# A fifth set of half products for queries and decays of heads 2 to 5, turned by transposes

## The chip, the cores and the metric

The kernel runs on one core of a Trainium2 chip. The metric is device time in microseconds (us) from start to end of one execution; of several runs the median is given. TensorE (PE in the rows) multiplies matrices, VectorE (DVE) and ScalarE (ACT) work element by element, GpSimd (POOL) does small vector work and starts transfers, SyncE (SP) starts transfers.

## What is computed

A decoder trunk of two layers on 512 positions with 2048 features. The first layer (a convolution branch and a latent-attention branch) is not touched. The second one is touched: one input projection, a gated linear recurrence (HGRN2) of 16 heads with a state of 128x128, an output projection, and the final norm.

```
p = h @ od_w_in[j]
q, f_raw, i_val, g = _split(p, [HGRN_FDIM, HGRN_FDIM, D_MODEL, D_MODEL])
o = hgrn2(q, f_raw, i_val, lb_all[l], hgrn_norm_g[j]) * jax.nn.silu(g)
x = x + o @ od_w_out[j]
```

In `hgrn2` each head has a query q, a decay that comes from f_raw through a sigmoid and a lower bound (so that the key is one minus the decay), and values i_val. Its output is a masked product of queries and keys with decays between them, plus what the state carries, normalised for each head and multiplied by the gate path of g.

## The kernel before

**Matmuls.** Every fp32 operand is split into a high and a low part (`split_plain`, `split_scaled`), and `mm3` (L223) makes one product of three matmuls: high by high, high by low, low by high. `dense` (L239) makes one result tile of 128 features by 512 positions from 16 blocks of 128 input features: four quarters of 12 matmuls. After each quarter `tick()` runs the hooks and lets every open chain take one step. A tick is thus the unit of the interleave: the order of TensorE's instructions is the order in which the program is written (`manual_schedule` for PE), while the tile framework orders the other engines itself.

**Sets of half products.** For values (`oi`) and gates (`og`) of the second layer, the 16 heads' columns are made in four sets (`SETS`) of 1024 columns each, by a scheme with seven products of half-size blocks in place of eight (`product`, `result`, the loop over `s_`, L936). One set is 7 products of 48 matmuls; the operands are sums and differences of blocks of the weights, formed on VectorE and ScalarE from blocks loaded into a ring (`ws`, tile `rw`). Here a result has positions in rows and features in columns, and is written to HBM (`vd`, `gd`).

**Heads.** Queries (`oq`) and decays (`of`) come from `dense`, so with features in rows. Heads 0 and 1 are made before the sets and kept in HBM (`qd`); heads 2 to 15 are made after the sets, one head each eight ticks, straight into SBUF: q into a tile with two buffers, the decay's key kn by turns into the tile kn and the tile m (`qk_tiles`).

**Chains.** `hgrn(h, ...)` (L1039) is the recurrence of one head, written as a generator with a `yield` for each tick that it lets pass. In order: f, products of f over groups of 4 (pi, xe; L1042 to L1054) and reciprocals; queries and keys scaled (qb, rc, X, ks; L1064 to L1078); the first product (L1082) and its masked copy into `at` (L1083); a first group of strip products (L1031) with masked copies (L1002), scaling of X (L1035) and ks (L1037); a second such group; transposes of the scaled keys (L1095); products with the values (L1101, L1111, L1113); norm, gate (L1127), and transposes back (L1131). The last step splits the head's output for the output projection.

`begin_chain` (a hook) starts the next chain when its head is projected and 8 to 10 ticks have passed; it loads the head's gate and values (`start`) as it starts. `SPREAD` places parts of the output projection (`w_out`, which adds each product to the residual xall, L671) between the dense results of heads 6 to 12; two more parts stand at the end.

**Loads.** Weight tiles of the heads' stage (`Loaded`) take two transfers from GpSimd's queue for each two quarters: the tile itself (wh), and once more added onto its negated high part (wl). Gates, values, residual and results go through SyncE's queue, which takes them in order.

Of the kernel before, what the change touches and what calls it, by code (L numbers as in the profile page):

```python
# [7 lines left out]
F32 = mybir.dt.float32  # L8
# [3 lines left out]
AF = mybir.ActivationFunctionType  # L12
# [3 lines left out]
P = 128  # L16
S = 512
# [8 lines left out]
RATE = 0.67  # L26
RATE0 = 0.4
MAN = "PE"
N_WTILES = 224
N_EARLY = 128  # L30
LAST = 2 * N_WTILES - NK
SETS = [("oi", 0), ("oi", 1), ("og", 0), ("og", 1)]


V_EVG, V_ODG, V_FING = 0, 16, 32
# [14 lines left out]
def trunk(ctx: ExitStack, tc: tile.TileContext, x, w, ws, vec, cst, rope, msk, out, order):  # L50
    nc = tc.nc
# [19 lines left out]
    def tmp(name="t", bufs=None):  # L71
        if name == "c":
            return tpc[0].tile([P, S], F32, name=name, tag=tpc[1])
        return tp.tile([P, S], F32, name=name, tag=name, bufs=bufs)
# [4 lines left out]
    def spawn(gen):  # L79
        chains.append(gen)  # L80
        return gen
# [157 lines left out]
    def dense(name, col, h, nk=NK):  # L239
        ps = ps_mm()  # L240
        for q in range(nk // 4):
            quarter(ps, next_quarter((name, col, q)), h, q, nk)
            tick()
        return ps
# [68 lines left out]
    with tc.tile_pool(name="x0", bufs=1) as x0:  # L313
# [29 lines left out]
        ident = cs[:, 0:P]  # L343
# [302 lines left out]
    def load_xa(src):  # L646
        for k in range(NK):
            nc.sync.dma_start(xa[k], src[:, k, :])
            yield
            yield  # L650
# [28 lines left out]
    h1 = []  # L679
# [86 lines left out]
    def decay(h, ps, kn):  # L766

        z = tmp("z")
        dve.tensor_tensor(out=z, in0=ps, in1=rb1, op=ALU.mult)
        t = tmp("th", bufs=1)  # L770
        act.activation(t, z, AF.Tanh, scale=0.5)
        act.activation(kn, t, AF.Identity, scale=la[:, h:h + 1], bias=nla[:, h:h + 1])
        return kn
# [91 lines left out]
            split_scaled(u[:, j, :H], vs[:, V_ODG + k:V_ODG + k + 1], h1[k][0][:, H:], h1[k][1][:, H:])  # L865


    qd = [dr.tile([P, 2, S], F32, name=f"qd{h}") for h in range(2)]
    for h in range(2):
        ps = dense("oq", h, h1)  # L870
        if h == 0:
            for k in range(4):
                x_sums(k)
            finish(c1)
        z = tmp("z")
        act.activation(z, ps, AF.Copy)
        nc.sync.dma_start(qd[h][:, 0, :], z)
        ps = dense("of", h, h1)
        if h == 0:
            for k in range(4, 8):  # L880
                x_sums(k)
            xctx.close()
            xtx.close()
            ph.append(sctx.enter_context(tc.tile_pool(name="ph", bufs=1, reuse_waits="tile")))
        nc.sync.dma_start(qd[h][:, 1, :], decay(h, ps, tp.tile([P, S], F32, name="gate", tag="gate", bufs=2)))
# [30 lines left out]
    vd = [dr.tile([P, 4, S], F32, name=f"vd{g}") for g in range(4)]  # L916
    gd = [dr.tile([P, 4, S], F32, name=f"gd{g}") for g in range(4)]

    def result(s_, col, b, in0, in1):

        name, a = SETS[s_]
        o = tp.tile([P, S], F32, name="z", tag="z") if b % 2 == 0 else tp.tile([P, S], F32, name="gate", tag="gate", bufs=2)
        dve.tensor_tensor(out=o, in0=in0, in1=in1, op=ALU.add)
        if name == "oi":
            act.activation(o, o, AF.Copy, scale=r1[:, b:b + 1])
        else:

            t = tmp("th", bufs=1)
            act.activation(t, o, AF.Tanh, scale=rh[:, b:b + 1])
            dve.scalar_tensor_tensor(out=o, in0=t, scalar=1.0, in1=o, op0=ALU.add, op1=ALU.mult)  # L930
        nc.sync.dma_start((vd if name == "oi" else gd)[2 * a + col][:, b, :], o)
# [1 line left out]
    def keep(tag, b):  # L933
        return ph[0].tile([P, S], F32, name=tag, tag=f"{tag}{b}")

    for s_ in range(4):  # L936
        p1, p2 = banks(), banks()
        for m in range(4):
            product(p1, "A11", m)
# [26 lines left out]
            result(s_, 1, b, p3[b], u[b])  # L966
        for b in range(2):
            result(s_, 1, 2 + b, p7[b], u[b])
        if s_ == 3:
            restore()  # L970
        p4 = banks()
        for m in range(4):
# [10 lines left out]
    def hgt(name, shape=(P, S), tag=None):  # L983
        return hg.tile(list(shape), F32, name=name, tag=tag or name)
# [54 lines left out]
    def hgrn(h, kn, q, gate, vr):  # L1039
# [49 lines left out]
        ab2 = hgt("ab2", (P, 4, 8))  # L1089
        yield from radix4(at, X, ks, t32, 32, ab2, P + 192)  # L1090
        yield
        yield
        pt = ps_x()
        for g in range(3):
            pe.transpose(pt[:, blocks(g)], ks[:, blocks(g)], ident)  # L1095
# [39 lines left out]
    heads = []  # L1135
    qk = {}

    def qk_tiles(h):
        qk[h] = (hg.tile([P, S], F32, name="q", tag="q", bufs=2), tmp("m", bufs=1) if h % 2 else hgt("kn"))
        return qk[h]  # L1140

    def start(h):
        gate = tp.tile([P, S], F32, name="gate", tag="gate", bufs=2)
# [3 lines left out]
        q, kn = qk[h]  # L1147
        heads.append(spawn(hgrn(h, kn, q, gate, vr)))

    for h in range(2):  # L1150
        for i, t in enumerate(qk_tiles(h)):
            nc.sync.dma_start(t, qd[h][:, i, :])


    SPREAD = {0: [(6, 1, 3), (7, 0, 3), (7, 1, 3), (8, 0, 3), (8, 1, 2), (9, 0, 2)],
              1: [(9, 1, 3), (10, 0, 3), (10, 1, 3), (11, 0, 3), (11, 1, 2), (12, 0, 2)]}
    begun = [2]
    since = [99]

    def begin_chain():  # L1160
        since[0] += 1
        n = len(heads)
        if n < begun[0] and since[0] >= (8 if n < 5 else 10 if n < 12 else 8):
            since[0] = 0
            start(n)

# [9 lines left out]
                    w_out("ow", list(range(4 * g, 4 * g + 4)), range(c, c + part[2]))  # L1176
                c += part[2]

    for h in range(2, 16):
        if h == 4:  # L1180
            spawn(load_xa(xd))
        ps = dense("oq", h, h1)
        q, kn = qk_tiles(h)
        act.activation(q, ps, AF.Copy)
        out_part(h, 0)
        decay(h, dense("of", h, h1), kn)
        begun[0] = h + 1
        out_part(h, 1)
    w_out("ow", [8, 9, 10, 11], range(NK))
# [87 lines left out]
def _weights(inp, order):  # L1277
# [26 lines left out]
        w[n // 2, :, n % 2] = b.transpose(1, 0, 2)  # L1304
    ws = np.zeros((len(SETS), 2, 2, 4, P, 2, S), np.float32)
    for n, (name, a) in enumerate(SETS):
        c0 = {"oi": 4096, "og": 6144}[name] + a * 1024

        b = od[:, c0:c0 + 1024].reshape(2, 4, 2, P, 2, S)
        ws[n] = b.transpose(0, 4, 1, 3, 2, 5)  # L1310
    return w.reshape(N_WTILES, P, 2 * S), ws.reshape(len(SETS), 2, 2, 4, P, 2 * S)

# [26 lines left out]
```

## Time and profile before

| what | us |
|---|---|
| median of 3 runs | 1762.09 |
| their range | 1756.79 to 1762.53 |
| profiled execution | 1758.25 |
| its span, first to last instruction | 1756.5 |
| TensorE busy / VectorE / ScalarE / GpSimd | 1732.9 / 1175.9 / 744.8 / 228.2 |

Stages by the trace: up to some 800 us the first layer, then heads 0 and 1, the four sets from about 860 to 1148, the heads up to about 1680, and the end. A row of the timeline has the start (us from the span's start), the duration, the engine, the line of kernel.py, the operation, output<-input, shapes and count; in brackets idle time of the engine before it and what ended it. Several instructions of one kind in a row may be merged into one row (x8: the passes of four fp32 products). The duration of a matmul runs from its start to its modelled end; since matmuls are pipelined, what one costs is read from start to start.

### The profile page before, as it was taken

The page shows a single profiled execution, that of the slowest core. Times are in us where ns is not written, and L with a number is a line of the kernel's source. Part 1 is how long each engine was busy: PE and PEld are TensorE (multiplying, and loading weights), DVE is VectorE, ACT ScalarE, POOL GpSimd, SP SyncE. Part 2 cuts the span into 40 slices and gives each one's busy share as a digit, 9 for nine tenths or more (in the row PEclk, how much of TensorE's full clock was granted, in tenths as well). Part 3 has the DMA queues.
Part 4 walks back from the last instruction along what each step waited for, and adds up shares of the span by engine and source line. Part 5 has one row for each costly group of instructions (what it writes and reads, how often), then busy time and mean ns, then how long its engine had stood idle before and what let it go on. Part 6 is the DMA issues. An engine that isn't in the chain of part 4 may idle for free.

```text
span 1756.5 us, 22385 instructions
## 1 busy us (share of the span) xinstructions
PE 1732.9 (99%) x8227; PEld 1437.6 (82%) x8227; DVE 1175.9 (67%) x2301; ACT 744.8 (42%) x1361; POOL 228.2 (13%) x307
## 2 busy tenths in 40 slices
PE   8999999999999999999999999999999999999997
PEld 6888888888888888887788888888888888888896
DVE  8554948494879885575777778876465555446656
ACT  6434444444342233275555455533433333333354
POOL 6000000000000000052000000022222222222200
PEclk9999999999999999999999999999999999999998
DMA  6222222222273223268777776798777787877642
GB/s 235 96 89 83 87 92 89 96 85 90 87 243 108 96 96 102 85 193 244 240 221 218 239 216 216 214 276 178 163 173 167 165 179 162 179 173 169 150 133 96
DMA packets 101805, 273.35 MB, mean 156 GB/s; under 512 B 9536, under 2 KB 31296, under 8 KB 101312
## 3 DMA queue, kind: packets, MB, share of 16 engines
q1 hardware_dynamic: 74048, 172.39, 29.3%
q0 software_dynamic: 27072, 98.58, 26.3%
q8 instruction: 64, 1.05, 0.3%
q10 hardware_dynamic: 576, 0.97, 0.2%
q14 instruction: 45, 0.37, 0.1%
HBM read 250.93 MB, written 20.97 MB: 155 GB/s over the span
## 4 chain that ended last, share of the span: by engine, by line
PE 92%; DVE 3%; issue 2%; DMA 2%; ACT 1%; POOL 0%; POOLq 0%; DVEq 0%; ACTq 0%
PE mm L225 25%; PE mm L227 25%; PE mm L226 25%; PE aux L1031 2%; PE aux L226 2%; PE aux L225 2%; PE aux L227 2%; PE aux L461 1%; PE aux L1082 1%; PE aux L1111 1%; DVE hl L249 1%; DMA rw<-ws 1%; PE aux L1113 1%; PE aux L1101 1%; DVE wq L253 1%
## 5 line engine op out<-in xcount | busy, mean ns | idle before, releaser
L252 ACT ACTIVATE wq<-raw 128x512 fp32r<-128x512 f32 x256 | 160.9, 631 | 346.2 <-PE mm L227 332.3
L225 PE MATMUL mm<-hh,wq 128*128 128x512 f32 x656 | 263.1, 401 | 1.1 <-ACT wq L252 1.1
L253 DVE TENSOR_TENSOR wq<-raw,wq 128x512 fp32r<-128x512 f32 x256 | 183.5, 719 | 120.2 <-ACT wq L252 119.6
L227 PE MATMUL mm<-hh,wq 128*128 128x512 f32 x656 | 257.5, 392 | 2.8 <-DVE wq L253 2.8
L226 PE MATMUL mm<-hl,wq 128*128 128x512 f32 x656 | 256.7, 391 | 0.0
L225 PE MATMUL mm<-hh,wh 128*128 128x512 f32 x512 | 207.8, 406 | 0.0
L227 PE MATMUL mm<-hh,wl 128*128 128x512 f32 x512 | 200.3, 391 | 0.0
L226 PE MATMUL mm<-hl,wh 128*128 128x512 f32 x512 | 199.6, 390 | 0.0
L510 DVE SCALAR_TENSOR_TENSOR y<-u,cwh,y 128x512 f32<-128x512 f32 x240 | 178.2, 747 | 2.4
L170 ACT ACTIVATE wl<-wh 128x1024 fp32r<-128x1024 f32 x86 | 91.5, 1064 | 178.4 <-PE mm L227 169.8
L227 PEld LDWEIGHTS mm<-hh,wq 128*128 128x128 f32 x656 | 123.8, 189 | 30.4 <-DVE wq L253 3.9
L225 PEld LDWEIGHTS mm<-hh,wq 128*128 128x128 f32 x656 | 124.3, 190 | 27.2 <-ACT wq L252 2.0
L226 PEld LDWEIGHTS mm<-hl,wq 128*128 128x128 f32 x656 | 124.2, 189 | 26.0 <-DVE hl L249 0.5
L227 PEld LDWEIGHTS mm<-hh,wl 128*128 128x128 f32 x512 | 96.1, 188 | 21.2 <-DMA wl<-w 0.4
L226 PEld LDWEIGHTS mm<-hl,wh 128*128 128x128 f32 x512 | 96.4, 188 | 17.8
L225 PEld LDWEIGHTS mm<-hh,wh 128*128 128x128 f32 x512 | 96.4, 188 | 17.5
L671 DVE TENSOR_TENSOR xall<-xall,mm 128x512 f32<-128x512 f32 x96 | 65.7, 684 | 64.3 <-PE mm L227 64.3
L252 ACT ACTIVATE wh<-rw 128x1024 fp32r<-128x1024 f32 x66 | 69.8, 1058 | 79.4 <-PE aux L227 23.7
L225 PE MATMUL mm<-mh,wq 128*128 128x512 f32 x256 | 101.6, 397 | 0.0
L226 PE MATMUL mm<-ml,wq 128*128 128x512 f32 x256 | 101.3, 396 | 0.0
L227 PE MATMUL mm<-mh,wq 128*128 128x512 f32 x256 | 101.2, 395 | 0.0
L253 DVE TENSOR_TENSOR wl<-rw,wh 128x1024 fp32r<-128x1024 f32 x66 | 79.8, 1221 | 20.2 <-ACT wh L252 6.0
(317 smaller groups left out, 3575.7 us busy)
## 6 DMA issues: line engine op xcount, KB each, us to landing
raw<-w SPq DMA_DIRECT2D x127, 512.0 KB, 3.3
rw<-ws SPq DMA_DIRECT2D x96, 512.0 KB, 4.7
wh<-w POOLq DMA_DIRECT2D x86, 512.0 KB, 3.7
wl<-w POOLq DMA_DIRECT2D x86, 512.0 KB, 6.2
ts<-ws POOLq DMA_DIRECT2D x16, 512.0 KB, 5.8
xall<-xT SPq DMA_DIRECT2D x16, 256.0 KB, 5.2
xd<-xall SPq DMA_DIRECT2D x16, 256.0 KB, 2.5
vr<-vd SPq DMA_DIRECT2D x16, 256.0 KB, 4.3
```

Source lines behind the costliest of these rows:

```text
L170: act.activation(self.lo, self.hi.bitcast(F32), AF.Copy, scale=-1.0)
L225: pe.matmul(ps, a[0][:, asl], b[0][:, bsl], start=first, stop=False)
L226: pe.matmul(ps, a[0][:, asl], b[1][:, bsl], start=False, stop=False)
L227: pe.matmul(ps, a[1][:, asl], b[0][:, bsl], start=False, stop=last)
L249: dve.scalar_tensor_tensor(out=lo, in0=src, scalar=g, in1=hi.bitcast(F32), op0=ALU.mult, op1=ALU.subtract)
L252: act.activation(hi, src, AF.Copy)
L253: dve.tensor_tensor(out=lo, in0=src, in1=hi.bitcast(F32), op=ALU.subtract)
L461: pe.matmul(po[:, jb * P:], vr[:, jb, blocks(j)], pts[jb], start=jb == 0, stop=jb == 3)
L510: dve.scalar_tensor_tensor(out=y, in0=u[:, j:j + S], scalar=cwh[:, w0 + j:w0 + j + 1], in1=y, op0=ALU.mult, op1=ALU.add)
L671: dve.tensor_tensor(out=xa[c], in0=xa[c], in1=ps, op=ALU.add)
L1031: pe.matmul(ps[:, i * 192:(i + 1) * 192], ks[:, blocks(g)], rhs, start=True, stop=True)
L1082: pe.matmul(ps[:, blocks(g)], kb[:, blocks(g)], qb[:, blocks(g)], start=True, stop=True)
```

## The change

`SETS` gets a fifth entry `qf`: the columns of queries and decays of heads 2 to 5. Its results (positions in rows) go to a new HBM tensor `qs`, queries as they are, decays after a tanh on ScalarE. Their dense results fall away, and with them 16 of the 224 weight tiles. When such a head is due, `load_qk` loads its two tiles and three ticks later `turn_qk` turns them: four 128x128 transposes each on TensorE, and a copy by ScalarE (for the decay with its scale and bias).

Dense results after the sets begin with head 6. Heads 6 to 13 now go to HBM (`qd`) and come back by `load_qk`; heads 14 and 15 stay in SBUF. kn is one tile for all of these. A chain begins 7 ticks after the one before, at the earliest 4 ticks after its load. One `yield` between the second group of strip products and the transposes of the keys is gone. `SPREAD` moves to heads 10 to 13.

```diff
-N_WTILES = 224
+N_WTILES = 208
-SETS = [("oi", 0), ("oi", 1), ("og", 0), ("og", 1)]
+SETS = [("oi", 0), ("oi", 1), ("og", 0), ("og", 1), ("qf", 0)]
+ENTRY = (0, 1)
...
     def result(s_, col, b, in0, in1):
...
+        if name == "qf":
+            if col:
+                act.activation(o, o, AF.Tanh, scale=rh[:, b:b + 1])
+            nc.sync.dma_start(qs[col][:, b, :], o)
+            return
...
-    for s_ in range(4):
+    for s_ in range(len(SETS)):
...
         yield from radix4(at, X, ks, t32, 32, ab2, P + 192)
         yield
-        yield
         pt = ps_x()
...
-    def qk_tiles(h):
-        qk[h] = (hg.tile([P, S], F32, name="q", tag="q", bufs=2), tmp("m", bufs=1) if h % 2 else hgt("kn"))
-        return qk[h]
+    def load_qk(h):
+        qk[h] = (hg.tile([P, S], F32, name="q", tag="q", bufs=2), hgt("kn"))
+        if not 2 <= h < 6:
+            for i, t in enumerate(qk[h]):
+                nc.sync.dma_start(t, qd[h][:, i, :])
+            return
+        rows.extend((tmp("z"), tmp("m", bufs=1)))
+        for i, t in enumerate(rows):
+            nc.sync.dma_start(t.rearrange("p (b c) -> p b c", b=4), qs[i][:, :, blocks(h - 2)])
+
+    rows = []
+
+    def turn_qk(h):
+
+        for i, t in enumerate(rows):
+            pt = ps_x()
+            for b in range(4):
+                pe.transpose(pt[:, blocks(b)], t[:, blocks(b)], ident)
+            if i == 0:
+                act.activation(qk[h][0], pt, AF.Copy)
+            else:
+                act.activation(qk[h][1], pt, AF.Identity, scale=la[:, h:h + 1], bias=nla[:, h:h + 1])
+        rows.clear()
...
-    SPREAD = {0: [(6, 1, 3), (7, 0, 3), (7, 1, 3), (8, 0, 3), (8, 1, 2), (9, 0, 2)],
-              1: [(9, 1, 3), (10, 0, 3), (10, 1, 3), (11, 0, 3), (11, 1, 2), (12, 0, 2)]}
-    begun = [2]
-    since = [99]
+    SPREAD = {0: [(10, 1, 4), (11, 0, 6), (11, 1, 6)],
+              1: [(12, 0, 4), (12, 1, 4), (13, 0, 8)]}
+    begun = [6]
+    loaded = [0]
+    since = [9]
 
     def begin_chain():
         since[0] += 1
         n = len(heads)
-        if n < begun[0] and since[0] >= (8 if n < 5 else 10 if n < 12 else 8):
+        loaded[0] += 1
+        if n not in qk and n < begun[0] and since[0] >= 3:
+            load_qk(n)
+            loaded[0] = 0
+        if rows and loaded[0] >= 3:
+            turn_qk(n)
+        if n in qk and since[0] >= 7 and loaded[0] >= (4 if n < 13 else 5 if n == 13 else 0):
             since[0] = 0
             start(n)
...
-    for h in range(2, 16):
-        if h == 4:
+    for h in range(6, 16):
+        if h == 8:
             spawn(load_xa(xd))
+
+        late = h >= 14
         ps = dense("oq", h, h1)
-        q, kn = qk_tiles(h)
-        act.activation(q, ps, AF.Copy)
+        z = hg.tile([P, S], F32, name="q", tag="q", bufs=2) if late else tmp("z")
+        act.activation(z, ps, AF.Copy)
+        if not late:
+            qd[h] = dr.tile([P, 2, S], F32, name=f"qd{h}")
+            nc.sync.dma_start(qd[h][:, 0, :], z)
         out_part(h, 0)
-        decay(h, dense("of", h, h1), kn)
+        kn = decay(h, dense("of", h, h1), hgt("kn") if h == 15 else tmp("m", bufs=1))
+        if late:
+            qk[h] = z, kn
+        else:
+            nc.sync.dma_start(qd[h][:, 1, :], kn)
```

Where instructions stand now is shown at three places. Lines of the changed kernel are 1 to 8 higher at the same step: L1031, L1035, L1037 became L1039, L1043, L1045.

VectorE, chain of head 8, between the scaling behind the first group of strip products and that behind the second (L1037, now L1045, on ks with the small factors ab of 4x96). Before, nothing but masked copies stands there:

```order
L1016 TENSOR_TENSOR X<-X,ab 128x4x64
L1017 TENSOR_TENSOR X<-X,ab 128x4x32
L1002 COPY_PREDICATED at<-mk,aux 128x2x96
L1002 COPY_PREDICATED at<-mk,aux 128x2x64
L1002 COPY_PREDICATED at<-mk,aux 128x2x96
L1002 COPY_PREDICATED at<-mk,aux 128x2x32
L1002 COPY_PREDICATED at<-mk,aux 128x2x64
L1035 TENSOR_TENSOR X<-X,ab_11799 128x4x96
L1002 COPY_PREDICATED at<-mk,aux 128x2x32
L1037 TENSOR_TENSOR ks<-ks,ab_11799 128x4x96
```

And now (kn, xe, pi, qb are the next head's):

```order
L1080 TENSOR_TENSOR rc<-kn,rc 128x64x4
L1082 TENSOR_TENSOR xe<-xe,pi 128x64x4
L1083 TENSOR_TENSOR pi<-pi 128x64x4
L1085 TENSOR_TENSOR X<-q,pi 128x512
L1010 COPY_PREDICATED at<-mk,aux 128x2x96
L1024 TENSOR_TENSOR X<-X,pi 128x16x16
L1010 COPY_PREDICATED at<-mk,aux 128x2x64
L1010 COPY_PREDICATED at<-mk,aux 128x2x96
L1010 COPY_PREDICATED at<-mk,aux 128x2x32
L1010 COPY_PREDICATED at<-mk,aux 128x2x64
L1043 TENSOR_TENSOR X<-X,ab_12293 128x4x96
L1010 COPY_PREDICATED at<-mk,aux 128x2x32
```

The front of the next head's chain moved ahead of the copies and scalings of this one.

TensorE, chain of head 1, around the second group of strip products (X, ks). Before:

```order
L225 MATMUL mm<-hh_6473,wh 128x512
L226 MATMUL mm<-hl_6474,wh 128x512
L227 MATMUL mm<-hh_6473,wl 128x512
L1031 MATMUL aux<-X,ks 128x192 x4
L225 MATMUL mm<-hh_6502,wh 128x512
```

And now, where z and m hold the queries and decays of head 2 in rows by time:

```order
L226 MATMUL mm<-hh_6367,wh 128x512
L227 MATMUL mm<-hl_6368,wh 128x512
L228 MATMUL mm<-hh_6367,wl 128x512
L1162 MATMUL aux<-cs,z 128x128 x4
L1162 MATMUL aux<-cs,m 128x128 x4
L1039 MATMUL aux<-X,ks 128x192 x4
L226 MATMUL mm<-hh_6394,wh 128x512
```

The two groups of the turn stand in front of the strip products in the chains of heads 1 to 4. Behind the strip products, 24 dense matmuls stood before the transposes of the keys, and 12 stand there now.

SyncE's queue, transfers for the chains of heads 4 to 6 (before) and 7 to 9 (now). Before, only values and gates:

```order
L1146 DMA vr<-vd_6980 128x4x128
L1144 DMA gate<-gd_6984 128x4x128
L1146 DMA vr<-vd_6980 128x4x128
L1144 DMA gate<-gd_6984 128x4x128
L1146 DMA vr<-vd_6980 128x4x128
L1144 DMA gate<-gd_6984 128x4x128
```

And now:

```order
L1149 DMA q<-qd_10573 128x512
L1149 DMA kn<-qd_10277 128x512
L1220 DMA qd_11638<-z 128x512
L1173 DMA vr<-vd_6980 128x4x128
L1171 DMA gate<-gd_6984 128x4x128
L1149 DMA kn<-qd_10573 128x512
L1149 DMA q<-qd_10891 128x512
L1173 DMA vr<-vd_6981 128x4x128
```

Loads of q and kn, and writes of heads still being projected, stand between them.

## Rows read from the trace of the kernel before

**Rows 1.** The page: engines, the chain that ended last, the residual's additions, busy us and mean ns

```profile
PE 1732.9 (99%) x8227; PEld 1437.6 (82%) x8227; DVE 1175.9 (67%) x2301; ACT 744.8 (42%) x1361; POOL 228.2 (13%) x307
...
PE 92%; DVE 3%; issue 2%; DMA 2%; ACT 1%; POOL 0%; POOLq 0%; DVEq 0%; ACTq 0%
...
L671 DVE TENSOR_TENSOR xall<-xall,mm 128x512 f32<-128x512 f32 x96 | 65.7, 684 | 64.3 <-PE mm L227 64.3
```

**Rows 2.** Timeline, ScalarE, set stage: start, duration, line, operation

```profile
937.20 0.60 ACT L945 ACTIVATE v<-aux 128x512 f32<-128x512 f32 x1 [3.69 <-PE aux L227]
...
1013.36 0.60 ACT L945 ACTIVATE v<-mm 128x512 f32<-128x512 f32 x1 [3.69 <-PE mm L227]
...
1089.80 0.60 ACT L945 ACTIVATE v<-mm 128x512 f32<-128x512 f32 x1 [3.29 <-PE mm L227]
```

**Rows 3.** Busy time by stretch, heads' stage: stretch, length, engines, clock, DMA share, GB/s

```profile
1158.80:1187.00 28.20, 28.20 (x147) 24.27 (x147) 15.76 (x56) 9.33 (x24) 7.44 (x12) 1.00 1.09 316
...
1215.00:1243.60 28.60, 28.60 (x150) 24.58 (x150) 17.09 (x56) 11.03 (x28) 7.67 (x13) 1.00 0.73 166
```

**Rows 4.** Timeline, TensorE, the chain of head 3 and the next chain's first product

```profile
1243.46 1.05 PE L1082 MATMUL aux<-qb,rc 128*128 128x128 f32 x8
...
1247.09 0.60 PE L1131 MATMUL aux<-cs,on 128*128 128x128 f32 x4
...
1247.52 1.47 PE L1031 MATMUL aux<-X,ks 128*128 128x192 f32 x8
...
1254.29 1.46 PE L1031 MATMUL aux<-X,ks 128*128 128x192 f32 x8
...
1255.46 0.53 PE L225 MATMUL mm<-hh,wh 128*128 128x512 f32 x1
...
1255.82 0.40 PE L226 MATMUL mm<-hl,wh 128*128 128x512 f32 x1
...
1261.05 0.49 PE L1095 MATMUL aux<-cs,ks 128*128 128x128 f32 x3
...
1271.88 1.05 PE L1082 MATMUL aux<-qb,rc 128*128 128x128 f32 x8
```

**Rows 5.** Timeline, VectorE, the same chain; the last row is the next head's

```profile
1254.87 0.42 DVE L1072 TENSOR_TENSOR rc<-kn,rc 128x256 f32<-128x256 f32 x1
...
1255.21 0.42 DVE L1074 TENSOR_TENSOR xe<-xe,pi 128x256 f32<-128x256 f32 x1
...
1258.93 0.55 DVE L1037 TENSOR_TENSOR ks<-ks,ab 128x384 f32<-128x384 f32 x1
...
1261.58 0.69 DVE L1078 TENSOR_TENSOR ks<-kn,xe 128x512 f32<-128x512 f32 x1 [1.00 <-PE aux L1095]
```

**Rows 6.** Busy time in the stretch from the mask copy to the keys' scaling

```profile
1245.51:1259.48 13.97, 13.97 (x70) 12.02 (x69) 13.33 (x43) 4.63 (x8) 2.83 (x4) 1.00 0.75 166
```

**Rows 7.** Timeline, chain of head 8: first product and the keys' second scaling

```profile
1408.84 1.05 PE L1082 MATMUL aux<-qb,rc 128*128 128x128 f32 x8
...
1421.95 0.55 DVE L1037 TENSOR_TENSOR ks<-ks,ab 128x384 f32<-128x384 f32 x1
```

**Rows 8.** DMA issues, 1158 to 1187 us: count, KB each, us to landing

```profile
xall<-xd SPq DMA_DIRECT2D x11, 256.0 KB, 13.5
...
wl<-w POOLq DMA_DIRECT2D x4, 512.0 KB, 8.1
```

**Rows 9.** DMA queues and issues, 1187 to 1243 us: packets, MB, share

```profile
q0 software_dynamic: 2349, 8.51, 70.4%
...
q1 hardware_dynamic: 2492, 1.27, 7.8%
...
wl<-w POOLq DMA_DIRECT2D x8, 512.0 KB, 6.1
```

**Rows 10.** DMA issues of the whole span: the one load of kn

```profile
kn<-qd SPq DMA_DIRECT2D x1, 256.0 KB, 4.5
```

## What the change will do to the time

> **What bounds the kernel now.** I read the page first: TensorE is busy 1732.9 of 1756.5 us and holds 92% of the chain that ended last [rows 1]. An average over stages proves nothing for one stage, so I went on to the stretches that the change touches. One is the stage of half products: the copies of the first product's result come once in each set, at 937.20, 1013.36 and 1089.80 us [rows 2], so a set lasts 76.16 and 76.44 us. It has 7 products of 48 matmuls, 336 in all, hence 0.227 us for each: dense matmuls back to back. The other is the stage of heads. In two of its stretches TensorE is busy for all of 28.20 and 28.60 us while VectorE has 15.76 and 17.09 [rows 3]. So in both stages TensorE's own work sets the time, and what the change takes off TensorE counts in full, unless a new wait eats it.
>
> For such waits I followed one head's chain through the trace, counted from its first product (L1082 at 1243.46). TensorE's own schedule is plain: the second group of strip products (L1031) comes at 1254.29, the first dense matmul behind it at 1255.46, the next at 1255.82, and after 24 dense matmuls the transposes of the keys (L1095) at 1261.05 [rows 4]. What those transposes need is the last scaling of the keys (L1037), which VectorE starts at 1258.93 and ends 0.55 us later [rows 5], so 16.02 us after the chain's first product; TensorE comes for it at 17.59. The slack is 1.57 us. It is no idle engine that makes this so late: in the 13.97 us up to that end VectorE was busy 13.33 [rows 6]. The reader is to see that VectorE is 60% busy on average and yet full in just the stretch for whose result TensorE comes.
>
> **The change, part by part.**
>
> *Products for dense work.* Heads 2 to 5 lose two dense results each, 8 x 48 = 384 matmuls; the fifth set adds 336. All run at the 0.227 us of [rows 2]: -87.1 + 76.2 = **-10.9 us**. I take the fifth set at the price of the others because all of its inputs arrive the same way; its results need no gate product on VectorE.
>
> *Transposes.* The set gives rows by time, the chain wants them by feature, so TensorE turns 4 heads x 2 tiles, four 128x128 transposes each. The nearest row is the same thing: L1131 starts at 1247.09 and the next group at 1247.52, 0.43 us [rows 4]. Eight groups: **+3.5 us**. The upper bound is the price of the strip products, 1254.29 to 1255.46, 1.17 us for a group [rows 4], 9.4 us in all. The lower end is no smaller than the 3.5, since TensorE has no idle time in which a turn could hide.
> The Trainium skill ("TensorE: Matmul & The Clock Gate", Part 4: PE-mode transpose) gives about 275 ns for one 128x128 transpose inside a kernel. By that the 32 transposes would be an estimated 8.8 us, and the sum 5.3 us later. The trace has 0.43/4 = 0.11 us for each, so I do not take it.
>
> *Chains seven ticks apart, and one tick less before the keys' transposes.* The work of a chain does not change. Its start moves: a tick is 12 dense matmuls, and chains that stood 8 to 10 ticks apart (and more where a head was not yet projected) now stand 7 apart, because 32 ticks of dense work are gone while 16 chains remain. From the period of 28.42 us at 8 ticks (1243.46 to 1271.88 [rows 4]) one tick of 12 x 0.227 = 2.72 goes: 25.7 us. VectorE's 17.09 us in such a chain [rows 3], plus about three and a half additions to the residual of 0.684 us [rows 1], still fits, so VectorE becomes no bound on average.
> But the dropped tick lies between the second strip group and the keys' transposes. There, TensorE now comes after 12 dense matmuls instead of 24. One behind a group costs 0.36 us, the rest (1261.05 - 1255.82)/23 = 0.227 each [rows 4]: 1255.46 + 0.36 + 11 x 0.227 = 1258.32, or 14.86 us after the first product, against a result that is ready at 16.02. **If VectorE keeps its order, TensorE waits 1.16 us there.** Whether it does is told by the order of the changed kernel (the first place shown with the change). For heads 1 to 4, 12, 14 and 15 the next chain's front stands behind the scaling or is short, or the turn's 0.9 us delays TensorE as well; a chain of before with that order had its scaling done at 1422.50, 13.66 us after its first product [rows 7], and that is in time. For heads 0, 5 to 11 and 13 the next chain's front stands ahead, as in the chain of [rows 5]. I walked those nine orders with the steps of [rows 5], 0.34 us from one small product to the next (1254.87 to 1255.21), and 0.6 for an addition to the residual. Heads 5 and 9 have the same fifteen products ahead as the chain that I measured: 1.2 us each. Heads 7 and 8 have one or two fewer and an extra piece: 1.0 each. Heads 6, 10 and 11 have three to five fewer, but two additions more: 0.7 each. Heads 0 and 13 have no gating in front: 0.5 each. The sum is 2.4 + 2.0 + 2.1 + 1.0 = **+7.5 us**. The low end is 0, if all behave as in [rows 7]; the high end is nine times 1.2 plus the 0.3 us that three of them may miss at the second strip group, 12 us. I keep the walk, since the row that it starts from is the same code in the same order.
>
> *Loads.* Queries and decays now travel through HBM for all heads but 14 and 15: at most two writes and two reads of 256 KB more for each chain. In the undisturbed stretch of two chains the hardware queue moved four loads of 256 KB in 7.8% of 56 us, 1.1 us each, and eight pairs of weights took 70.4%, 4.9 us a pair [rows 9]. A chain of 7 ticks then takes 3.5 x 4.9 + 2 x 1.1 + 4 x 1.1 = 23.8 us of the DMA engines out of 25.7 to 26.9, some 90%. That is priced at 0, because it has a cover: in [rows 3] the first stretch ran with a DMA share of 1.09, weights landing in 8.1 us instead of 6.1 [rows 8, 9], and TensorE lost nothing.
>
> The sum is -10.9 + 3.5 + 7.5 = **+0.1 us**: the gain of the half products is paid back, a third by the turns and the rest at one hand-over. Against the profiled execution of 1758.25 us (a span of 1756.5 and 1.75 around it) this gives 1758.4. The three runs of before lie between 1756.79 and 1762.53 with the median at 1762.09, so the profiled one is among their low ones; I name 1760, half way between 1758.4 and that median moved by the same 0.1 us.
>
> **The rivals.**
> *A, no wait at the transposes.* The scaling comes early in every chain as in [rows 7], because what stands ahead on VectorE finds gaps that I count as filled. For it: only 15.76 to 17.09 us of each chain are busy. Against it: the 13.33 of 13.97 us in [rows 6]. Then -10.9 + 3.5 = -7.4: about 1751 for the profiled execution, 1754.7 from the median. With half of the waits it is 1755 to 1758.
> *B, a load that holds VectorE.* Slower than before. In place of two alternating tiles the decays (kn) have one. Its next load can start when L1078's successor has read it, some 18 us after a chain's first product (1261.58 [rows 5]), and VectorE's first step of the next chain stands in order right behind the mask copy, 2.7 us after that chain's first product. That leaves 26.9 + 2.7 - 18.8 = 10.8 us. The one such load in the trace landed in 4.5 us [rows 10], but loads in a crowded queue took 13.5 [rows 8]. From 10.8 us on, every later us stands in front of everything on VectorE, the strip products wait too, and a landing of 13.5 costs 2.7 us in each of up to eight chains. With half of them late that is 11 us: 1769.
> *C, dear turns.* If a group of four transposes costs the 1.17 us of a strip group, the sum grows by 5.9 us: 1764 from the profiled execution. The skill's 275 ns, named above, would give 5.3.
> *D, the set is not the price of the others.* It stands last, where tiles for the heads are opened; were it held by its loads, 336 matmuls could take 80 us: +4, 1762. Against it: the sets of [rows 2] differ by 0.28 us.
>
> **How the numbers follow.** Forecast (within 4 us of no change): 0.47. A: 0.31. B: 0.16. C: 0.03. D: 0.03. A measurement of this kernel tells 0.3%, 5.3 us, from no change. A gives faster; half of A's milder part is already in the forecast; I add 0.01 from the forecast's low edge: faster 0.32. B and C are slower, with 0.02 of D and the forecast's high edge: slower 0.21. Same: 0.47. The range runs from 1750, which takes in A read from the profiled execution, to 1769, B's time. The likeliest case's own range is 1755 to 1764.
>
> **What would show it.** Right: the list of what TensorE waits for has a new head, the transposes of the keys waiting for VectorE's scaling of ks, nine or so times with 0.5 to 1.3 us, some 7 us in all; chains about 26 to 27 us apart; a set period of 76 us five times; turn groups of 0.4 us. Wrong in direction A: chains 25.7 us apart and TensorE free of that wait. Wrong in direction B: VectorE idle ahead of the first step of a chain (f from kn), released by a DMA, and the strip products waiting too. What I would have misjudged then is the walk through VectorE's order, the one part of the sum that no single row shows.

## The result, and the profile after

The changed kernel takes 1772.13 us (median of 4 runs, 1771.99 to 1773.62) against 1761.89 us for the kernel before in the same comparison: ratio 1.0068, interval 1.0056 to 1.0080. A second comparison (below) gave 1.0077 (1.0061 to 1.0092). By these intervals it is slower by 10 to 16 us; the forecast was no change, 1760, and its range ended at 1769.

The page of the profiled execution (span 1770.2 us) against [rows 1]: the part of the span in which TensorE is not busy rose from 23.6 to 38.9 us. The chain that ended last breaks off early on this page (its shares add up to some 16% of the span), so it measures nothing here; that VectorE has 4 of the 16 only points to a place.

```profile
span 1770.2 us, 22549 instructions
...
PE 1731.3 (98%) x8211; PEld 1431.8 (81%) x8211; DVE 1224.6 (69%) x2351; ACT 762.3 (43%) x1379; POOL 208.5 (12%) x279
```

The view that decides is the list of what TensorE waited for in the heads' stage, 1150 to 1700 us: engine, tile and line, what it waited for, us in total, times, longest.

```profile
PE aux L1102 <- DVE ks L1045: 9.0, 9, 1.8
PE aux L1138 <- DVE on L1134: 2.0, 1, 2.0
PE aux L1039 <- DVE X L1025: 1.5, 5, 0.5
PE mm L228 <- DMA wl<-w: 1.0, 1, 1.0
```

The first row is the wait that the prediction named: nine times, eight of them in the chains that it named, and 9.0 us where it said 7.5. The second and third were not in its sum.

The half products behave as those of [rows 2]: ScalarE's copies of the first product now give four periods, 80.89, 76.20, 76.74 and 76.36 us. The long one is the first, and no effect of the change: the kernel before has it too, 81.00 us from a first copy that [rows 2] leave out (the first row here is of before, the others of the changed kernel).

```profile
856.20 1.06 ACT L945 ACTIVATE v<-mm 128x512 f32<-128x512 f32 x2
...
859.71 1.06 ACT L953 ACTIVATE v<-mm 128x512 f32<-128x512 f32 x2
...
940.60 0.60 ACT L953 ACTIVATE v<-aux 128x512 f32<-128x512 f32 x1 [3.70 <-PE aux L228]
...
1016.80 0.60 ACT L953 ACTIVATE v<-mm 128x512 f32<-128x512 f32 x1 [3.69 <-PE mm L228]
...
1093.54 0.60 ACT L953 ACTIVATE v<-mm 128x512 f32<-128x512 f32 x1 [3.59 <-PE mm L228]
...
1169.90 0.60 ACT L953 ACTIVATE v<-mm 128x512 f32<-128x512 f32 x1 [3.70 <-PE mm L228]
```

From start to start in TensorE's timeline, the matmuls of the five sets take 389.5 us (387.8 in the profile of run 8), where those of the four took 312.1: the fifth set adds 75.7 to 77.4 us, priced at 76.2.

The turns cost what was priced as well. In TensorE's timeline the two groups of head 2 start 0.43 and 0.44 us before what follows them, as L1131 in [rows 4]:

```profile
1289.45 0.60 PE L1162 MATMUL aux<-cs,z 128*128 128x128 f32 x4
1289.88 0.60 PE L1162 MATMUL aux<-cs,m 128*128 128x128 f32 x4
1290.32 1.84 PE L1039 MATMUL aux<-X,ks 128*128 128x192 f32 x8
```

That is 0.11 us for each 128x128 transpose, from start to start. The duration of one is another number, 0.27 us up to its modelled end, here the least, the median and the greatest of 16:

```profile
L1162 PE MATMUL aux<-cs,z x16: 270/272/273, 1289.4 to 1370.4; 128*128 128x128 f32 x16
```

The Trainium skill ("TensorE: Matmul & The Clock Gate", Part 4: PE-mode transpose) has about 275 ns for a bf16 one inside a kernel. The trace agrees with that as a duration, 0.27 us; as the price of one in a group it is too high, and the measured 0.11 decides. Two of the four strip groups behind a turn are also 0.37 us longer than the others (1290.32 to 1291.86 for the one shown, where [rows 4] have 1.17), so that the four turns come to some 4.2 us.

**The chain that waits.** Head 5, whose first product starts at 1385.89, answers to the chain of [rows 4] and [rows 5]. VectorE:

```profile
1387.76 0.69 DVE L1134 TENSOR_TENSOR on<-on,gate 128x512 f32<-128x512 f32 x1 [2.30 <-ACT on L1133]
1388.37 0.68 DVE L672 TENSOR_TENSOR xall<-xall,mm 128x512 f32<-128x512 f32 x1
1388.96 0.74 DVE L1091 COPY_PREDICATED at<-mk,aux 128x512 f32<-128x512 uint8 x1
...
1396.92 0.29 DVE L1025 TENSOR_TENSOR X<-X,ab 128x128 f32<-128x128 f32 x1
...
1402.33 0.55 DVE L1045 TENSOR_TENSOR ks<-ks,ab 128x384 f32<-128x384 f32 x1
```

and TensorE, which comes for X at 1397.35 after a wait, and for ks at 1403.03 after another of 1.39 us:

```profile
1385.89 1.06 PE L1090 MATMUL aux<-qb,rc 128*128 128x128 f32 x8
...
1397.35 1.54 PE L1039 MATMUL aux<-X,ks 128*128 128x192 f32 x8 [0.42 <-DVE X L1025]
...
1401.02 0.39 PE L227 MATMUL mm<-hl,wh 128*128 128x512 f32 x1
1401.24 0.39 PE L228 MATMUL mm<-hh,wl 128*128 128x512 f32 x1
1403.03 0.52 PE L1102 MATMUL aux<-cs,ks 128*128 128x128 f32 x3 [1.39 <-DVE ks L1045]
```

Behind the gating (L1134) stands an addition to the residual, so the mask copy (L1091) starts 3.07 us after the first product. ks is ready 16.99 us after the first product, where the prediction had 16.02, and the transposes start another 0.15 us later.

**Head 0** waits longest, 1.8 us. The front of head 1 stands in VectorE's queue ahead of head 0's scaling, and it waits itself, for ScalarE's copy (L1057), which stands behind a weight tile that came late:

```profile
1252.29 0.41 DVE L1050 TENSOR_SCALAR f<-kn 128x512 f32<-128x512 f32 x1
1255.83 0.39 DVE L1060 TENSOR_TENSOR pi<-pi,f 128x128 f32<-128x128 f32 x1 [3.13 <-ACT pi L1057]
```

```profile
1253.06 1.06 ACT L171 ACTIVATE wl<-wh 128x1024 fp32r<-128x1024 f32 x1 [5.75 <-DMA wh<-w]
1254.02 0.61 ACT L772 ACTIVATE th<-z 128x512 f32<-128x512 f32 x1
1254.67 0.81 ACT L773 ACTIVATE m<-th,nla,la 128x512 f32<-128x512 f32 x1
1255.39 0.41 ACT L1057 ACTIVATE pi<-f 128x128 f32<-128x128 f32 x1
```

**Head 12** meets rival B, at this one place. Head 13's decay is written to HBM and read back just before its chain starts; f waits for it, and the norm (rs) and the gating (on) of head 12 stand behind f:

```profile
1603.60 0.43 DVE L1050 TENSOR_SCALAR f<-kn 128x512 f32<-128x512 f32 x1 [6.67 <-DMA kn<-qd]
1603.94 0.15 DVE L1126 SCALAR_TENSOR_TENSOR rs<-ss,er 128x4 f32<-128x4 f32 x1
...
1606.80 0.69 DVE L1134 TENSOR_TENSOR on<-on,gate 128x512 f32<-128x512 f32 x1 [0.21 <-ACT on L1133]
```

TensorE waits 2.0 us for `on`. In the profile of the second comparison the same load landed 6.6 us after its issue instead of 3.8, and the wait was 5.1 us.

### The profile page after: what moved, and what is told of

Same layout as the page of the kernel before. It is cut to its first block, busy times and chain, and to the rows that moved or that the text cites. A ratio compares the mean times of both kernels' runs of the same rounds, so it can differ in the third digit from the quotient of the medians.

```text
span 1770.2 us, 22549 instructions
## 1 busy us (share of the span) xinstructions
PE 1731.3 (98%) x8211; PEld 1431.8 (81%) x8211; DVE 1224.6 (69%) x2351; ACT 762.3 (43%) x1379; POOL 208.5 (12%) x279
## 5 line engine op out<-in xcount | busy, mean ns | idle before, releaser
L226 PE MATMUL mm<-hh,wh 128*128 128x512 f32 x384 | 156.6, 408 | 0.0
L228 PE MATMUL mm<-hh,wl 128*128 128x512 f32 x384 | 150.8, 393 | 1.1 <-DMA wl<-w 1.0
L227 PE MATMUL mm<-hl,wh 128*128 128x512 f32 x384 | 150.1, 391 | 0.0
L171 ACT ACTIVATE wl<-wh 128x1024 fp32r<-128x1024 f32 x70 | 74.1, 1058 | 131.0 <-PE mm L228 111.7
L253 ACT ACTIVATE wh<-rw 128x1024 fp32r<-128x1024 f32 x82 | 86.7, 1059 | 96.2 <-PE aux L228 30.1
L254 DVE TENSOR_TENSOR wl<-rw,wh 128x1024 fp32r<-128x1024 f32 x82 | 99.2, 1221 | 22.3 <-ACT wh L253 8.0
L254 DVE TENSOR_TENSOR wl<-ts,wh 128x1024 fp32r<-128x1024 f32 x60 | 72.2, 1221 | 31.0 <-ACT wh L253 19.6
L228 PEld LDWEIGHTS mm<-hh,wl 128*128 128x128 f32 x384 | 72.3, 188 | 17.6 <-DMA wl<-w 1.9
L226 PE MATMUL mm<-wh,hh 128*128 128x512 f32 x216 | 84.0, 389 | 0.0
```

The lines of the kernel that those rows point to most:

```text
L171: act.activation(self.lo, self.hi.bitcast(F32), AF.Copy, scale=-1.0)
L226: pe.matmul(ps, a[0][:, asl], b[0][:, bsl], start=first, stop=False)
L227: pe.matmul(ps, a[0][:, asl], b[1][:, bsl], start=False, stop=False)
L228: pe.matmul(ps, a[1][:, asl], b[0][:, bsl], start=False, stop=last)
L253: act.activation(hi, src, AF.Copy)
L254: dve.tensor_tensor(out=lo, in0=src, in1=hi.bitcast(F32), op=ALU.subtract)
```

## The experiments

All were compared with the kernel before on the same chip, in three further comparisons. The theory: VectorE executes its queue in the order in which the scheduler wrote it, the next head's front stands ahead of what TensorE needs next, and every wait on it is TensorE's loss. The rivals: a dear turn, a set or loads dearer than priced, or loss in the stages that the change leaves alone.

**1. The fronts held back.** Nothing is added or left out; the first step of a chain's front is ordered behind the last scaling of ks.

```diff
+        scaled[0] = dve.tensor_tensor(out=k4[:, :, 0:3, :], ...
...
+        with tc.issue_after(scaled[0].ins) if scaled[0] is not None else ExitStack():
             dve.tensor_scalar(f, kn, ...
```

> The changed kernel, with one thing more: on VectorE the first step of a chain (f from kn) is queued behind the second scaling of the keys of the chain before it, so that no part of the next chain's front can stand ahead of that scaling. No work is added or removed. Theory (VectorE's order at the one-tick hand-over costs the time): the waits of the keys' transposes for the scaling (9.0 us in 9 waits) fall below 1 us, those of the strip products for X (1.5 us) below 0.5, and the time falls from 1772.1 by 10 to 13 us to 1759 to 1762. Rival (VectorE has too much to do in seven ticks, so what is taken from one hand-over is lost at the next): the waits appear at the chain's first product or at the products with the values, and the time stays at 1769 or above.

1755.77 us, ratio 0.9986 (0.9975 to 0.9998): 0.0082 below the changed kernel's ratio, some 14 us, more than expected, and no slower than the kernel before. Waits of TensorE, 1150 to 1700 us:

```profile
PE aux L1141 <- DVE on L1137: 4.9, 1, 4.9
PE mm L228 <- DMA wl<-w: 0.8, 1, 0.8
```

The waits for ks and X are gone, all of them, and head 12's is left. The theory holds, and the rival does not: no wait appears at the first product or at the products with the values.

**2 and 3. The dropped tick.** The changed kernel with the `yield` back, and the kernel before with only the `yield` dropped.

> The changed kernel with the dropped tick between the second strip products and the keys' transposes put back; chains still 7 ticks apart. Theory (the dropped tick exposes the scaling): the waits at the keys' transposes fall from 9.0 us to below 1, and the time to 1762 to 1766, because the last chain now ends a tick later, with up to 3 us at the end that nothing hides. Rival (the spacing of seven ticks alone makes VectorE late): the waits go on, at this place or the next, and the time stays at 1769 or above.

> The kernel before, with only that tick dropped: chains 8 to 10 ticks apart, dense work as before. Theory: the keys' transposes come 14.86 us after the first product; in the chains of heads 0 to 4 the scaling ends near 16.0, so five waits of 1.2 to 1.4 us appear there, 6 us in all, and none in the other heads, where it ends at 13.7 to 14.8; the time goes from 1761.9 to 1767 to 1768. Rival (the wait needs the chains 7 ticks apart): no waits, 1762.

With the tick back: 1764.34 us, ratio 1.0038 (1.0024 to 1.0051). The waits for ks are gone, but head 12's is 7.4 us, and the chains end a tick later (from the last chain's first product to the transposes of the final norm it is 62.7 us where the changed kernel has 59.1). That the time is inside the expected 1762 to 1766 is in part luck, since the expectation had not reckoned with a longer wait at head 12. The kernel before without the tick: 1764.53 us, ratio 1.0037 (1.0024 to 1.0050), 7 us slower, near the 5 to 6 us that were expected. That is luck as well: of the 6 us of waits for ks expected in five chains there are 2.8 in seven, and the rest are at the output transposes (these two rows, and 0.9 us for `on`), since VectorE's order changed with the tick:

```profile
PE aux L1094 <- DVE ks L1037: 2.8, 7, 1.1
PE aux L1130 <- DVE ab L1022: 2.6, 2, 1.3
```

The kernel before has no wait for ks with the tick and seven without it; the changed kernel has nine without it and none with it. So the dropped tick brings these waits in both kernels; putting it back is no cure.

**4. No turns.** ScalarE copies the unturned tiles, so heads 2 to 5 compute something else.

```diff
-            pt = ps_x()
-            for b in range(4):
-                pe.transpose(pt[:, blocks(b)], t[:, blocks(b)], ident)
...
-                act.activation(qk[h][0], pt, AF.Copy)
+                act.activation(qk[h][0], t, AF.Copy)
```

> The changed kernel without the turn: the rows by time of queries and decays of heads 2 to 5 are copied as they are, so TensorE makes no transposes for them (the part left out; those heads compute something else). ScalarE's two copies stay. If a turn costs what the trace of the changed kernel shows, 0.87 us for a head's two groups, and 0.7 us in all for the waits of the strip products behind two of them, the time falls by 3.5 to 5 us to 1767 to 1768.6. If each group cost the 1.17 us of a strip group, it would fall by 9.4 us to 1762.7.

A miss: 1777.81 us, ratio 1.0120 (1.0105 to 1.0135), slower although work is left out. Without the turn the fronts of heads 2 to 5 are ready earlier, and the scheduler puts them, too, ahead of the scaling:

```profile
PE aux L1102 <- DVE ks L1045: 12.3, 12, 1.8
PE aux L1138 <- DVE on L1134: 6.2, 1, 6.2
PE aux L1120 <- ACT st L1110: 4.9, 2, 3.1
PE aux L1039 <- DVE X L1025: 2.6, 5, 0.9
```

Twelve chains wait for ks instead of nine: the turn had guarded heads 2 to 4. The larger new loss is the third row. ScalarE's copies of the decay tile, which no longer wait for a transpose, stand early in its queue and wait there for their loads, 6.7 us in head 0's chain and 6.9 in head 2's, with the state copies (st) behind them; head 0's period grows from 28.04 to 34.50 us. This run can't price the turn.

**5. Head 12 mended as well.** As run 1, and head 13's front behind the gating of head 12.

```diff
+        gated[h] = dve.tensor_tensor(out=on, in0=on, in1=gate, op=ALU.mult)
...
+        behind = gated.get(h - 1, scaled[0])
+        with tc.issue_after(behind.ins) if behind is not None else ExitStack():
```

> The kernel after, with the first step of each chain's front (f from kn) queued on VectorE behind the last scaling of the keys of the chain before, as in the run with the fronts held back, and for head 13 alone behind the gating of head 12. No work is added. In that earlier run TensorE still waited 4.9 us once, at the output transposes of head 12, because the norm of head 12 stood on VectorE behind f of head 13, which waited for the load of kn. Theory (a late load held VectorE's queue, and nothing else does): that wait goes, head 12's period falls from 49.5 to about 44.5 us, and head 13's first product does not wait, since its front was done 9 us ahead of it. Time 5 us below the run with the fronts held back: the whole sum -10.9 + 3.5 = -7.4 us against the kernel before, ratio 0.996 (0.9945 to 0.9972). Rival (TensorE waits for head 13 in any case, as its load is late): the 4.9 us come back at head 13's first product, ratio 0.9986 again.

1751.79 us, ratio 0.9957 (0.9942 to 0.9971): faster than both kernels. Head 12's period falls from 49.48 us in run 1 to 42.55, by 6.9 where 5 were expected. One wait is left in the stage:

```profile
PE mm L228 <- DMA wl<-w: 0.7, 1, 0.7
```

This is the prediction's sum without waits, -7.4 us: by the ratio it is -7.6 us, with an interval from -10.2 to -5.1, so the agreement to 0.2 us is finer than the measurement.

**6. The same without turns.** Run 5 with the edit of run 4, to price the turn where VectorE's order is held.

> The kernel of the run before this one, without the 32 transposes on TensorE that turn queries and decays of heads 2 to 5: ScalarE copies the unturned tiles, so that those heads compute something else. With the order of VectorE held, taking the turns away can no longer let the fronts of heads 2 to 5 move ahead. Theory (turns cost TensorE's time alone, 0.87 us for a head): 3.5 us faster than with the turns, about 11 us below the kernel before, ratio 0.9938, chain periods of heads 1 to 4 at 25.8 to 26.2 instead of 26.6 to 27.0. Rival C (dear turns): 9.4 us faster, ratio 0.990. Rival (a new wait takes their place): within 1 us of the run with the turns.

A second miss: 1757.55 us, ratio 0.9987 (0.9976 to 0.9998), slower than with the turns. With VectorE's order held, ScalarE's queue is what is left of run 4: its copy of z stands early in the queue and waits 10.0 us for the load, and head 0's state product waits behind it. Head 3's output transposes wait behind a shorter one, 2.7 us for the other tile's load.

```profile
ACT q L1165 <- DMA z<-qs: 10.0, 1, 10.0
```

```profile
PE aux L1124 <- ACT st L1114: 5.9, 1, 5.9
PE aux L1142 <- DVE on L1138: 1.8, 1, 1.8
```

Where neither wait falls, the price can be read: from first product to first product, the chains of heads 1, 2 and 4 take 25.72, 25.72 and 25.83 us, with the turn 26.99, 26.63 and 26.74. That is 0.9 us for a head in two of them (1.3 in the first, where the strip group behind the turn is longer itself: 1.84 us in the row above, 1.47 in [rows 4]); dear turns would have been 2.3.

**7. Keys scaled ahead of X.** Two lines exchanged in the changed kernel; fronts stay ahead.

```diff
+        k4 = v4(ks)
+        dve.tensor_tensor(out=k4[:, :, 0:3, :], ...
         dve.tensor_tensor(out=x0[:, :, 1:4, :], ...
-        k4 = v4(ks)
-        dve.tensor_tensor(out=k4[:, :, 0:3, :], ...
```

> The kernel after, with the two last steps behind each pair of strip copies exchanged: ks is scaled ahead of X, the fronts stay where they are. Theory (TensorE waits at the keys' transposes for VectorE's queue, step for step): ks is ready 0.6 us earlier in each chain, X (which is wanted late in the second scaling) 0.5 later; nine waits of 1.0 us on average shrink to 0.4, so the waits for ks fall from 9.0 to about 4 us and the time by 4 to 5.5 us against the kernel after. Rival (ks is not held by what stands ahead in the queue, but by the strip products that the scaling follows): no change within 1 us.

1767.94 us, ratio 1.0046 (1.0032 to 1.0059), 4.9 us below the changed kernel on the same chip, as expected: a step that no longer stands ahead of ks in VectorE's queue is time that TensorE gets back. The waits at the keys' transposes are down from 9.0 to 2.0 us (listed as waits for a masked copy, which now ends last; 4 us were expected), those for X up from 1.5 to 3.3.

```profile
PE aux L1138 <- DVE on L1134: 4.3, 1, 4.3
PE aux L1039 <- DVE X L1025: 3.3, 7, 0.7
PE aux L1102 <- DVE at L1010: 2.0, 4, 0.9
```

**8. The changed kernel again**, beside runs 5 to 7.

> The kernel after, unchanged, beside the other three on the same chip. By its first comparison 1.0068 times the kernel before (1.0056 to 1.0080), so 10 to 14 us above it. Theory: again some 12 us, with 9 us of waits for ks, about 2 for X and the strip group, 2 at the output transposes of head 12. If part of the difference lay in the first layer, which the change does not touch, the stretch up to the accumulators' transposes (796.8 us in the profile of before, 799.1 in that of after) would be longer again by 2 us; if that is only scatter, it is not.

1772.80 us, ratio 1.0077 (1.0061 to 1.0092). The untouched first layer's mark stands at 796.0 us here, 796.8 in the profile of before and 799.1 in the first one of after: scatter, no loss of the change. The waits for ks and X are those of the first profile (9.0 us in nine, 1.5 in five); head 12's is longer:

```profile
PE aux L1138 <- DVE on L1134: 5.1, 1, 5.1
```

**9 and 10. One place each.** Only head 13's front behind the gating of head 12; only head 1's front behind the scaling of head 0.

> The kernel after, with one edge more on VectorE: the first step of head 13's chain (f from kn) is queued behind the gating of head 12; the fronts of all other heads stay ahead of the scaling. In the two profiles of the kernel after, TensorE waits there 2.0 and 5.1 us, and head 12's period is 46.3 and 49.8 us where the kernel with all fronts held has 42.6; behind the wait the granted clock stands at 0.50 for 3 to 4 us. Theory: this one place costs 3.8 to 7.2 us, so head 12's period is 42.6, the waits for ks stay at 9.0 us, and the time lies 4 to 7 us below the kernel after, ratio against the kernel before 1.0037 to 1.0055. Rival (the load of kn is late for head 13's own first product as well): the time is within 1.5 us of the kernel after.

> The kernel after, with the front of head 1 alone queued behind the last scaling of the keys of head 0. In the profile of the kernel after that front waits 3.1 us for ScalarE (its copy of f into pi stands behind a copy of weights and a tanh) and holds VectorE's queue for as long. Theory: head 0's period falls from 28.0 to 25.2 us, its wait for ks of 1.8 and for X of 0.55 are gone, all other heads keep theirs (7.2 us for ks), and the time falls by 2.8 us against the kernel after, ratio against the kernel before about 1.006. Rival (the wait moves to head 1's first product, since its front starts later): no change within 1 us.

Head 13 alone: 1765.23 us, ratio 1.0036 (1.0022 to 1.0050). Against the 1.0068 and 1.0077 of the changed kernel that is 5.6 to 7.2 us; head 12's period falls from 49.75 to 42.55 us, and the other waits stay:

```profile
PE aux L1105 <- DVE ks L1047: 9.0, 9, 1.8
PE aux L1041 <- DVE X L1027: 1.5, 5, 0.5
```

Head 1 alone: ratio 1.0061 (1.0049 to 1.0074), too near to the changed kernel's for the time to tell 2.8 us. The trace tells it: head 0's period falls from 28.03 to 25.24 us, and the waits for ks from 9.0 in nine chains to

```profile
PE aux L1105 <- DVE ks L1047: 7.3, 8, 1.4
```

The places add up. From first product to first product, the chains of run 8 are longer than those of run 5, where nothing waits, by 2.8 us (head 0), 9.9 (heads 5 to 11), 7.2 (head 12), 1.4 (heads 13 and 14), and by nothing in heads 1 to 4: 21.3 us, and the medians lie 21.0 apart.

## Why the prediction was wrong

**Right.** TensorE's time sets the end in both stages. The fifth set cost what was put for it, and so did the turns themselves (eight groups of 0.43 us); the 0.7 us of longer strip products behind them were not in the sum. What the 32 dropped ticks of dense work save stands in no single row, but with every wait taken away the kernel lands at -7.6 us (-10.2 to -5.1), where the two terms -10.9 and +3.5 give -7.4. The named wait came, at the named place, for the named reason, in eight of the nine chains and in one other. Loads priced at 0 held, but for two: head 13's decay, and the weight tile for which ScalarE's queue waits in head 0's chain.

**The step that failed is the third term of the sum, +7.5 for the walk through VectorE's order.** It should have been 18 us by the first profile of the changed kernel (its chains are 17.9 us longer than those of run 5) and 21 by the second, and four things make the difference.
- *What a chain waits for ks.* Walked: 0.5 (head 0), 1.2, 0.7, 1.0, 1.0, 1.2, 0.7, 0.7 (heads 5 to 11), 0.5 (head 13). Measured in run 8: 1.80; 1.37, 0.65, 0.53, 1.43, 1.38, 0.74, 0.43; none in head 13 and 0.64 in head 14. Heads 5, 8 and 9 are above the walk by 0.2 to 0.4 and have an addition to the residual ahead of the mask copy; heads 7 and 11 have none and are 0.3 to 0.5 below it. But heads 6 and 10 have one too and meet the walk, so this explains a part at most. Head 0 is off because the walk counted VectorE's own steps and not what VectorE itself waits for, ScalarE's copy (run 10). In all 9.0 against 7.5.
- *A wait costs more than it lasts.* Where TensorE waits 1.80 us for ks, the stretch is 1.99 us longer than in run 5, and so in each of the nine: 10.6 us for 9.0 of waits. Most of that is the way in which the list counts: from the modelled end of the matmul before, 0.39 us after its start, while without a wait the next one starts after 0.227 (the rows of head 5, 1401.02 to 1403.03). The walk reckoned from start to start, so 10.6 is what its 7.5 has to be held against. Of the 3.1 us between them 1.3 are the 0.15 us from the end of the scaling to the start of the transposes, nine times, which the walk put at nothing.
- *The strip products.* The prediction put 0.3 us in three chains, and that only into its high end. Measured: 1.5 us of waits for X in five chains, 2.7 us in length, and 0.2 us of length in each of heads 7 to 9, where no wait is listed.
- *Head 12*, 3.8 us in the first profile and 7.2 in the second, the largest single place. With 10.6 and 2.7 that is 20.5 of the 21.3 us; the rest are pieces of about 0.2. Rival B has the mechanism right, a late kn that holds VectorE's queue, but I looked for it in up to eight regular chains, behind the mask copy. It came in the one chain whose decay is still being projected as it is due: in the two profiles the write to HBM takes 4.8 and 5.1 us, the load behind it 3.8 and 6.6. What it held up was the norm and the gating of the head before.

**Rival A** (no wait) was not the changed kernel, but it is run 5: 1751.79 us where A had 1751 to 1754.7. **C** and **D** fell: 0.11 us a transpose, and 75.7 to 77.4 us for the fifth set. D's argument was weaker than it looked, since [rows 2] leave out the first set with its 81.00 us (the sets start at 835.7 us, not at 860).

The range failed with the term: its high end had B's 11 us on top of the walk's 7.5. In run 8 the walk's part is 6.6 us above its 7.5, and head 12 costs 7.2; added to 1758.4 neither alone would have passed 1769, but both came together.

What stays open: by how much the residual's additions alone lengthen the waits, since taking them away would move VectorE's order too, and why the weight tile in head 0's chain lands late. No run here shows either.

## What to carry to other kernels

Before a tick between a result and its use is dropped, read the queue of the engine that makes the result, with everything in it that itself waits (for another engine or a load), not only what is busy; a front of the next stage that is ready early and needed late can be ordered behind the result by an explicit edge, which here (with head 13's front behind a later step) was worth 21 us with no work removed. What a wait costs is read from start to start, not from the list of waits. A result that goes through HBM just before its use should not stand in a queue ahead of anything that TensorE needs sooner. And a run that leaves work out may be slower for the order that the scheduler then writes, so a price is read from stretches where the order is the same.

## What the runs showed of the hardware

The wait in head 12 cost more than itself. Busy time by stretches of 2 us in run 8: length, then TensorE, its weight loads, VectorE, ScalarE, GpSimd, then the granted clock.

```profile
1607.00:1609.00 2.00, 1.95 (x7) 1.78 (x8) 1.81 (x6) 0.83 (x2) 0.00 (x0) 0.50 0.72 249
1609.00:1611.00 2.00, 2.00 (x6) 1.51 (x6) 1.97 (x7) 0.91 (x2) 0.87 (x1) 0.50 0.39 115
1611.00:1613.00 2.00, 2.00 (x10) 1.65 (x9) 2.00 (x5) 0.26 (x2) 0.21 (x1) 0.96 0.72 78
```

After 5.1 us without work TensorE comes back at a granted clock of 0.50, the lower of its two levels (1.2 GHz), for some 4 us, and a dense matmul takes 0.43 us from start to start instead of 0.227. Of the 7.2 us of head 12 that is 1.6, and the transposes behind the wait take another 0.4. In the first profile of the changed kernel the wait was only 2.0 us, and the clock fell all the same:

```profile
1603.00:1605.00 2.00, 2.00 (x10) 1.67 (x9) 0.97 (x4) 0.75 (x2) 0.82 (x1) 1.00 1.06 206
...
1609.00:1611.00 2.00, 2.00 (x7) 1.51 (x5) 1.90 (x6) 1.31 (x2) 0.39 (x1) 0.50 0.46 135
```

Behind head 0's wait of 1.8 us, which ended at 1267.76, it stayed at 1.00:

```profile
1268.00:1270.00 2.00, 2.00 (x12) 1.65 (x11) 0.69 (x1) 1.44 (x2) 0.33 (x1) 1.00 0.98 364
```

The Trainium skill ("TensorE: Matmul & The Clock Gate", Part 1: The HAM clock gate) says that TensorE's clock is halved when the engine has been idle. These rows agree that it is halved, and show it behind a wait of 2.0 us, for which head 12's period is 3.8 us longer than in run 5.
